# Running sums of an output projection loaded two blocks ahead, and a norm's product moved from VectorE to GpSimd

## The chip, the cores and the metric

The kernel runs on one core of a Trainium2 chip. The metric is the device time of one execution in microseconds (us); of several runs, the median counts. Engine names in the profile: PE is TensorE's matmul and PEld its weight load, DVE is VectorE, ACT is ScalarE, POOL is GpSimd, and SPq is the queue of SyncE, which issues the DMAs.

## What is computed

The reference is a two-layer decoder trunk on 1024 tokens of width 1024, in float32. Layer 0 is retention with 4 heads (query and key width 256, value width 512), layer 1 is stick-breaking attention with 8 heads (query and key width 128, value width 256) on keys and values that are made once from layer 0's result. Cut to what matters here:

```python
u = rms_norm(h, ret_norm_pre)
q, k, v, g = split(u @ ret_w_in)
q = rope(q, pos); k = rope(k, pos) * RET_QK_DIM ** -0.5
o = retention_chunkwise(q, k, v)                # per head
mu = mean(o, -1); var = mean(square(o - mu), -1)
o = (o - mu) * rsqrt(var + EPS)                 # the retention norm
y = (merge_heads(o) * silu(g)) @ ret_w_out      # the output projection
h = h + rms_norm(y, ret_norm_post)
k_sh, v_sh = split(rms_norm(h, kv_norm) @ w_kv)
# layer 1
q, g = split(rms_norm(h, sb_norm_pre) @ sb_w_in)
o = stick_breaking_attention(q, k_sh, v_sh)
y = (merge_heads(o) * silu(g)) @ sb_w_out
return h + rms_norm(y, sb_norm_post)
```

## The kernel before

The work is cut into four phases: retention on tokens 0 to 511 (A, t=0) and 512 to 1023 (A, t=1), then stick-breaking on the same halves (C, t=0 and t=1). A phase takes four heads, or four pairs of heads in C, one after the other. Every product of float32 matrices is made of three matmuls (`mm3`, lines 110 to 112) on high and low parts, which `split` (lines 254, 255, with a scale 257, 258) makes on ScalarE and VectorE. Weights come by DMA in tiles `wraw` of 128x512 and are split into `whl`.

The instructions are not ordered by hand to the last: steps of the main chain (projections) and side chains (scores, mixing, norm, statistics) are merged into one program by `merge`, and a scheduler then orders the instructions of each engine when the kernel is built, by the times it expects. All DMAs concerned are issued from SyncE's queue, in order: where one of them must wait for a tile or for a result, those behind it wait too. Tiles come from pools that rotate: a tile's memory is used again when its last reader is done. The pool `f2` has six buffers of 128x512; running sums, squares and the rotary's products use it. The PSUM banks of projections are two called `ma` and two called `mb`.

The output projection, `outproj`, is a chain of 16 steps: eight blocks `c` of 128 output columns, in two halves of 6 matmuls. Each head adds its part to running sums `y_d[c]` in DRAM. For the first head ScalarE copies the block from PSUM; for later heads the sum so far is loaded into an `f2` tile, VectorE adds the block (L194 in the profile) and the tile is stored. In the last output projection of a phase (except the last phase, which ends in another function) the block's squares are added up too, by ScalarE (L219, L222) and GpSimd (L223). The banks go ma, ma, mb, mb over the blocks; the projection that comes next takes all four at its first step. The three places where a phase's last output projection meets the next phase's first projection are called boundaries here: 1 is near 440 us, 2 near 862 us, 3 near 1283 us. In the last head of a retention phase the first four steps of the head before it (blocks 0 and 1) stand ahead of the projection of values and gates, the rest behind it.

The retention norm is in `mix`, step `o(ib)`, once for each of 4 heads, 4 blocks of 128 tokens and 2 halves, 32 times: statistics on VectorE (L608, L609), variance plus epsilon and its reciprocal root on GpSimd (L611, L612), the product -mean x root on VectorE (L613), and then `normed` on ScalarE (L625), which runs one step later for all but the last block and takes the root as scale and the product as bias. After that come the gate's multiply (L652), transposes on TensorE (L656) and a split. Rotary's last operations on GpSimd are L396 and L397; the row sums' loads and all other DMAs show as L64, the helper's line.

Of the kernel before, what the change touches and what calls it, by code (L numbers as in the profile page):

```python
# [13 lines left out]
ALU = mybir.AluOpType  # L14
# [17 lines left out]
def trunk(ctx, tc, xT, wts, gains, trig, ident_in, cols, out):  # L32
# [13 lines left out]
    def S(tag, shape, dt=F32):  # L46
        cnt[0] += 1
        return sb.tile([128] + list(shape), dt, tag=tag, name=f"{tag}{cnt[0]}", bufs=BUFS[tag])

    def PS(tag):  # L50
        cnt[0] += 1
        return ps.tile([128, 512], F32, tag=tag, name=f"p{tag}{cnt[0]}", bufs=BUFS[tag])
# [4 lines left out]
    def hl(tag):  # L57
        return S(tag, [2, 512], F32R)

    def f32(ap):  # L60
        return ap.bitcast(F32)

    def dma(dst, src, eng=nc.sync):
        eng.dma_start(dst.bitcast(F32), src.bitcast(F32))  # L64

    keep = tc.keep_in_program_order
    V, A_, G, MM = nc.vector, nc.scalar, nc.gpsimd, nc.tensor.matmul
# [28 lines left out]
    def unit(idx, gain=None):  # L96

        w = S("whl", [2, 1024], F32R)
        for c in range(2):
            o = 512 * c  # L100
            raw = S("wraw", [512])
            dma(raw[:], wts[idx, :, o:o + 512])
            for a, b, g in [(p[0] - o, p[1] - o, p[2]) for p in gain if o <= p[0] < o + 512] if gain else [(0, 512, None)]:
                split((w[:, 0, o + a:o + b], w[:, 1, o + a:o + b]), raw[:, a:b], g)
        return w

    def mm3(p, lh, ll, rh, rl, start, stop, goes_on=False):

        kw = dict(skip_group_check=True) if goes_on else {}
        MM(p, lh, rh, start=start, stop=False, **kw)  # L110
        MM(p, lh, rl, start=False, stop=False, **kw)  # L111
        MM(p, ll, rh, start=False, stop=stop, **kw)  # L112
# [19 lines left out]
    def ahead(n, make):  # L132

        box = {}

        def get(u):
            if u < n and u not in box:
                box[u] = make(u)
            return box.get(u)
        return get  # L140
# [28 lines left out]
    def outproj(base, oT, y_d, first, acc=None, tags=None):  # L169

        box = {}
        get = ahead(4, lambda ng: unit(base + ng))

        def chunk(j):
            c, half = divmod(j, 2)
            ng, b = divmod(c, 2)
            w = get(ng)
            if j % 4 == LEAD:
                get(ng + 1)
            if half == 0:  # L180
                box["p"] = PS(tags[c % 4] if tags and c < 4 else banks4[c % 4])
                box["y"] = S("f2", [512])
                if not first:
                    dma(box["y"][:], y_d[c])
            p, y = box["p"], box["y"]
            for e in (2 * half, 2 * half + 1):
                n = slice(256 * e + 128 * b, 256 * e + 128 * b + 128)
                mm3(p[:], w[:, 0, n], w[:, 1, n], oT()[e][:, 0, :], oT()[e][:, 1, :], e == 0, e == 3)
            if half == 0:
                return  # L190
            if first:
                A_.activation(y[:], p[:], AF.Copy)
            else:
                V.tensor_tensor(y[:], p[:], y[:], ALU.add)  # L194
            dma(y_d[c], y[:])
            if acc is not None:
                sumsq(acc, y[:], c)

        return Chunks([lambda j=j: chunk(j) for j in range(16)], lambda: get(0))

    def merge(main, *sides, nxt=None):
# [14 lines left out]
    def sumsq(acc, src, c):  # L216
        if c == 0:
            acc.append(S("acc", [512]))
            A_.activation(acc[0][:], src, AF.Square)  # L219
        else:  # L220
            t = S("f2", [512])
            A_.activation(t[:], src, AF.Square)  # L222
            G.tensor_tensor(acc[0][:], acc[0][:], t[:], ALU.add)  # L223
# [36 lines left out]
    def flat(x):  # L260
        return x[:, :, :].rearrange("p a b -> p (a b)")
# [3 lines left out]
    y_d = [[dr.tile([128, 512], F32, tag=f"y{t}{c}", name=f"y{t}{c}") for c in range(8)] for t in range(2)]  # L265
# [135 lines left out]
    class AHead:  # L401
# [139 lines left out]
        def out(self, y_d, acc=None, tags=None):  # L541
            return outproj(self.base + 12, lambda: self.oT, y_d, self.h == 0, acc, tags)
# [33 lines left out]
        def mix(self):  # L576

            h, q = self.h, self.q
            self.on, self.state = [], []

            def state_out(d):
                p = PS("o")
                for tb in range(4):
                    n, kn, v = slice(128 * d, 128 * d + 128), self.kn[tb], self.v[tb]
                    mm3(p[:], kn[:, 0, n], kn[:, 1, n], v[:, 0, :], v[:, 1, :], tb == 0, tb == 3)
                s = hl("ko")
                gg = GAMMA[h] ** HT
                A_.activation(s[:, 0, :], p[:], AF.Copy, scale=gg)
                V.scalar_tensor_tensor(s[:, 1, :], p[:], gg, f32(s[:, 0, :]), ALU.mult, ALU.subtract)
                dma(st_d[h][d][:], flat(s))  # L590

            def state_in():
                for d in range(2):
                    s = hl("ko")
                    dma(flat(s), st_d[h][d][:])
                    self.state.append(s)

            def o(ib):
                p = PS("o")
                il = slice(128 * ib, 128 * ib + 128)  # L600
                for d, s in enumerate(self.state):
                    mm3(p[:], q[d][:, 0, il], q[d][:, 1, il], s[:, 0, :], s[:, 1, :], d == 0, False)
                for jb in range(ib + 1):
                    n = slice(128 * (ib - jb), 128 * (ib - jb) + 128)
                    sc, v = self.sc[jb], self.v[jb]
                    mm3(p[:], sc[:, 0, n], sc[:, 1, n], v[:, 0, :], v[:, 1, :], not self.state and jb == 0, jb == ib)
                bs, mv = S("small", [6]), S("small", [2])
                V.bn_stats(bs[:], p[:])  # L608
                V.bn_aggr(mv[:], bs[:])  # L609
                r, nb = S("small", [1]), S("small", [1])  # L610
                G.tensor_tensor(r[:], mv[:, 1:2], cc[:, 16 + 4 * h + ib:17 + 4 * h + ib], ALU.add)  # L611
                G.tensor_tensor(r[:], r[:], mhalf[:, 0:1], ALU.pow)  # L612
                V.scalar_tensor_tensor(nb[:], mv[:, 0:1], -1.0, r[:], ALU.mult, ALU.mult)  # L613
                late.append((ib, p, r, nb))
                if ib:
                    normed()

            late = []

            def normed():  # L620
                ib, p, r, nb = late.pop(0)
                if ib % 2 == 0:
                    self.on2 = S("sgn", [1024])
                on = self.on2[:, 512 * (ib % 2):512 * (ib % 2) + 512]
                A_.activation(on, p[:], AF.Identity, scale=r[:], bias=nb[:])  # L625
                self.on.append(on)

            os = [lambda ib=ib: o(ib) for ib in range(4)] + [normed]
            if self.t == 0:
                self.give = [lambda d=d: state_out(d) for d in range(2)]  # L630
                return os
            self.give = []
            return [state_in] + os
# [94 lines left out]
    class CPair:  # L728
# [43 lines left out]
        def out(self, y_d, acc=None):  # L772
            return outproj(self.base + 12, lambda: self.oT, y_d, self.pr == 0, acc)
# [345 lines left out]
```

## Time and profile before

| what | value |
|---|---|
| runs | 1802.1, 1799.63, 1802.94 us; median 1802.1 |
| profiled execution, its own time | 1795.14 us |
| its span | 1793.4 us |
| mean granted TensorE clock | 0.994 |
| DMA moved | 292.14 MB, mean 163 GB/s |
| loads of running sums | 96, 256 KB each |

A line of the timeline gives the start, the length, the engine, the program's line, the operation, out<-in with the tiles' names, the shape, and in brackets the engine's idle time before it with the instruction or transfer that ended it. A line of the waits gives who waited, for whom, how many us in total, how many times, and the longest. A group's line gives busy us and mean ns of one, then the idle time before. A line of the windows gives, for a stretch of time, the busy us of each engine with the number of instructions, the granted clock as a share of full speed, and the share of the DMA engines. Durations come from one profiled execution. Matmuls are pipelined, so one of 0.39 us may follow another after 0.23.

### The profile page before, as it was taken

Reading aid. Unit: us, or ns where it says so; the run is one execution under the profiler, and the core shown is the slowest. Engines: PE = TensorE matmul, PEld = TensorE weight load, DVE = VectorE, ACT = ScalarE, POOL = GpSimd, SP = SyncE. Lnnn points to the kernel's source line nnn. Section 1 sums busy time; section 2 is a strip of 40 time slices with the busy share of each in tenths; the row PEclk is TensorE's granted clock in tenths of the full one; section 3 lists DMA queues with packets and bytes.
Section 4 is the critical chain, followed back from the end, with each engine's and each line's share of the span. In section 5 each row is a group of like instructions: output and inputs, shape, how many; then the busy total and the mean of one; then the engine's idle time right before and its main releaser. Section 6 shows DMA issues by size and latency. Waiting matters only on the chain. (4 is left out here: it accounts for less than half of the span.)

```text
span 1793.4 us, 23629 instructions
## 1 busy us (share of the span) xinstructions
PE 1736.5 (97%) x8132; PEld 1432.5 (80%) x8132; DVE 1197.1 (67%) x1947; ACT 815.8 (45%) x1526; POOL 266.5 (15%) x345
## 2 busy tenths in 40 slices
PE   8999999999999899999999999999999999999997
PEld 6888788777788688777777888888787888888886
DVE  7757767887866868697475455557577456646675
ACT  6435546464444535363344443444344445344541
POOL 0210302201304210101131100000200010000103
PEclk9999999999999999999999999999999999999998
DMA  5225465557445646275664526344644442522243
GB/s 190 83 106 194 147 235 177 182 194 265 158 140 196 216 147 232 92 251 188 213 216 158 199 80 200 129 153 152 220 144 166 139 144 94 174 97 102 98 136 112
DMA packets 152553, 292.14 MB, mean 163 GB/s; under 512 B 17136, under 2 KB 19312, under 8 KB 152432
## 3 DMA queue, kind: packets, MB, share of 16 engines
q1 hardware_dynamic: 152432, 290.63, 47.8%
q8 instruction: 64, 1.05, 0.2%
q14 instruction: 57, 0.47, 0.1%
HBM read 233.93 MB, written 56.62 MB: 162 GB/s over the span
## 5 line engine op out<-in xcount | busy, mean ns | idle before, releaser
L255 DVE TENSOR_TENSOR whl<-wraw,whl 128x512 fp32r<-128x512 f32 x312 | 219.7, 733 | 62.6 <-ACT whl L254 62.4
L254 ACT ACTIVATE whl<-wraw 128x512 fp32r<-128x512 f32 x312 | 183.5, 623 | 106.5 <-PE pmb L112 47.6
L258 DVE SCALAR_TENSOR_TENSOR whl<-wraw,gn,whl 128x256 fp32r<-128x256 f32 (+1 forms) x256 | 150.7, 633 | 117.2 <-ACT whl L257 114.4
L257 ACT ACTIVATE whl<-wraw,gn 128x256 fp32r<-128x256 f32 (+1 forms) x256 | 142.6, 611 | 151.2 <-PE pmb L112 121.1
L110 PE MATMUL pma<-xh,whl 128*128 128x512 f32 x384 | 154.8, 403 | 7.3 <-DVE f L194 6.8
L110 PE MATMUL pmb<-xh,whl 128*128 128x512 f32 x384 | 153.3, 399 | 2.1 <-DVE sg L768 1.4
L111 PE MATMUL pma<-xh,whl 128*128 128x512 f32 x384 | 150.9, 393 | 0.0
L112 PE MATMUL pma<-xh,whl 128*128 128x512 f32 x384 | 150.8, 393 | 0.0
L112 PE MATMUL pmb<-xh,whl 128*128 128x512 f32 x384 | 150.7, 393 | 0.0
L111 PE MATMUL pmb<-xh,whl 128*128 128x512 f32 x384 | 149.9, 390 | 0.0
L798 POOL TENSOR_SCALAR_AFFINE_SELECT sgn<-sgn 128x128 f32<-128x128 f32 x64 | 25.1, 392 | 671.8 <-ACT sgn L793 559.3
L800 DVE TENSOR_TENSOR_SCAN sgn<-sgn 128x128 f32<-128x128 f32 (+3 forms) x64 | 89.0, 1391 | 45.5 <-POOL sgn L798 45.5
L255 DVE TENSOR_TENSOR AT<-pz,AT 128x512 fp32r<-128x512 f32 (+1 forms) x96 | 53.0, 554 | 71.4 <-ACT AT L254 71.0
L254 ACT ACTIVATE AT<-pz 128x512 fp32r<-128x512 f32 (+1 forms) x96 | 46.7, 486 | 111.1 <-PE pz L830 111.0
L110 PEld LDWEIGHTS pma<-xh,whl 128*128 128x128 f32 x384 | 72.9, 190 | 22.6 <-DVE f L194 7.4
L110 PEld LDWEIGHTS pmb<-xh,whl 128*128 128x128 f32 x384 | 72.3, 188 | 17.8 <-DVE sg L768 3.1
L112 PEld LDWEIGHTS pma<-xh,whl 128*128 128x128 f32 x384 | 72.7, 189 | 16.0
L112 PEld LDWEIGHTS pmb<-xh,whl 128*128 128x128 f32 x384 | 72.2, 188 | 15.9
L111 PEld LDWEIGHTS pma<-xh,whl 128*128 128x128 f32 x384 | 72.9, 190 | 13.2
L111 PEld LDWEIGHTS pmb<-xh,whl 128*128 128x128 f32 x384 | 72.4, 188 | 13.5
L111 PE MATMUL pma<-oT,whl 128*128 128x512 f32 x208 | 81.5, 392 | 1.2 <-DVE oT L255 1.2
L110 PE MATMUL pma<-oT,whl 128*128 128x512 f32 x208 | 82.2, 395 | 0.4 <-DVE f L194 0.4
(310 smaller groups left out, 4485.3 us busy)
## 6 DMA issues: line engine op xcount, KB each, us to landing
wraw<-in_wts_dram SPq DMA_DIRECT2D x624, 256.0 KB, 3.2
y<-f SPq DMA_DIRECT2D x120, 256.0 KB, 2.9
f<-y SPq DMA_DIRECT2D x96, 256.0 KB, 3.6
v<-v SPq DMA_DIRECT2D x16, 512.0 KB, 3.2
vo<-v SPq DMA_DIRECT2D x32, 256.0 KB, 2.8
A<-h SPq DMA_DIRECT2D x12, 512.0 KB, 4.5
st<-ko SPq DMA_DIRECT2D x8, 512.0 KB, 3.7
sg<-in_xT_dram SPq DMA_DIRECT2D x16, 256.0 KB, 2.9
```

Of the source, the lines that this page charges most:

```text
L110: MM(p, lh, rh, start=start, stop=False, **kw)
L111: MM(p, lh, rl, start=False, stop=False, **kw)
L112: MM(p, ll, rh, start=False, stop=stop, **kw)
L254: A_.activation(dst[0], src, AF.Copy)
L255: V.tensor_tensor(dst[1], src, f32(dst[0]), ALU.subtract)
L257: A_.activation(dst[0], src, AF.Copy, scale=scale)
L258: V.scalar_tensor_tensor(dst[1], src, scale, f32(dst[0]), ALU.mult, ALU.subtract)
L798: G.affine_select(n[:, dg], n[:, dg], [[-1, 128]], ALU.is_gt, 1.0, base=0, channel_multiplier=1)
L800: V.tensor_tensor_scan(n[:, :W][:, ::-1], n[:, :W][:, ::-1], n[:, :W][:, ::-1], 1.0, ALU.mult, ALU.bypass)
```

## The change

`outproj` gets a helper, `sums`, that makes the tile of a block once and, where it is not the first head, starts its load. At the first half of block c, the tiles of blocks c, c+1 and c+2 are asked for, so a load is issued up to two blocks before its block's matmuls; before, it was issued at its own block's first half. For the first head nothing is asked ahead. In `mix`, VectorE now negates the mean right behind the statistics (new tile `nm`), and GpSimd multiplies it by the reciprocal root behind its power; the product on VectorE goes. VectorE issues as many instructions as before, GpSimd 32 more; numbers of matmuls and DMAs stay the same.

```diff
@@ outproj
+        def sum_so_far(c):
+            y = S("f2", [512])
+            if not first:
+                dma(y[:], y_d[c])
+            return y
+        sums = ahead(8, sum_so_far)
+
         def chunk(j):
...
             if half == 0:
                 box["p"] = PS(tags[c % 4] if tags and c < 4 else banks4[c % 4])
-                box["y"] = S("f2", [512])
+                sums(c)
                 if not first:
-                    dma(box["y"][:], y_d[c])
-            p, y = box["p"], box["y"]
+                    sums(c + 1)
+                    sums(c + 2)
+            p, y = box["p"], sums(c)
@@ mix, o(ib)
                 V.bn_stats(bs[:], p[:])
                 V.bn_aggr(mv[:], bs[:])
+                nm = S("small", [1])
+                V.tensor_scalar(nm[:], mv[:, 0:1], -1.0, None, ALU.mult)
                 r, nb = S("small", [1]), S("small", [1])
                 G.tensor_tensor(r[:], mv[:, 1:2], cc[:, 16 + 4 * h + ib:17 + 4 * h + ib], ALU.add)
                 G.tensor_tensor(r[:], r[:], mhalf[:, 0:1], ALU.pow)
-                V.scalar_tensor_tensor(nb[:], mv[:, 0:1], -1.0, r[:], ALU.mult, ALU.mult)
+                G.tensor_tensor(nb[:], nm[:], r[:], ALU.mult)
```

## The prediction

> **What bounds the kernel now.** I read the page first, then the waits of TensorE's weight loads, then the timelines around the rows that name a running sum, then the windows.
>
> ```profile
> span 1793.4 us, 23629 instructions
> PE 1736.5 (97%) x8132; PEld 1432.5 (80%) x8132; DVE 1197.1 (67%) x1947; ACT 815.8 (45%) x1526; POOL 266.5 (15%) x345
> ```
>
> TensorE is busy for 97% of the span, and the change takes no matmul away. So only TensorE's gaps, 1793.4 - 1736.5 = 57 us, and stretches at a lower clock can be won. The waits of the weight loads over the whole span say how many of those gaps belong to a running sum (columns: us in total, times, longest):
>
> ```profile
> PEld pma L110 <- DVE f L194: 8.4, 5, 2.8
> PEld pmb L110 <- DVE f L194: 1.0, 1, 1.0
> ```
>
> Six waits, 9.4 us, for the add at L194. The timeline of the weight loads (start, length, in brackets the idle time before it) and the waits between 1250 and 1320 us show where they are:
>
> ```profile
> 441.75 0.19 PEld L110 LDWEIGHTS pma<-xh,whl 128*128 128x128 f32 x1 [2.75 <-DVE f L194]
> 447.38 0.19 PEld L110 LDWEIGHTS pmb<-xh,whl 128*128 128x128 f32 x1 [1.00 <-DVE f L194]
> 862.03 0.19 PEld L110 LDWEIGHTS pma<-xh,whl 128*128 128x128 f32 x1 [1.03 <-issue]
> 866.83 0.19 PEld L110 LDWEIGHTS pma<-xh,whl 128*128 128x128 f32 x1 [2.19 <-DVE f L194]
> PEld pma L110 <- DVE f L194: 2.4, 1, 2.4
> ```
>
> These are the three phase boundaries: the last output projection of a phase, followed by the first projection of the next, which wants the same PSUM banks. Between them they hold 2.75 + 1.00 + 1.03 + 2.19 + 2.4 = 9.4 us. (The 1.03 has no releaser; it is the same wait for a bank, so I count it. Two small waits elsewhere make up the 8.4.)
>
> Why the adds are late there is in SyncE's queue and on VectorE:
>
> ```profile
> 431.68 0.32 SPq L64 DMA_DIRECT2D y<-f  x1
> 432.09 0.38 SPq L64 DMA_DIRECT2D f<-y  x1
> ...
> 436.05 0.69 DVE L194 TENSOR_TENSOR f<-pma,f 128x512 f32<-128x512 f32 x1 [1.71 <-DMA f<-y]
> 441.00 0.69 DVE L194 TENSOR_TENSOR f<-pma,f 128x512 f32<-128x512 f32 x1 [3.66 <-DMA f<-y]
> ...
> 450.64 0.69 DVE L194 TENSOR_TENSOR f<-pmb,f 128x512 f32<-128x512 f32 x1 [3.31 <-DMA f<-y]
> ```
>
> The load of a block's sum is issued right behind the store of the sum before it, and the add waits for that load. It is a ring: store issued at 431.68, load at 432.09, add at 436.05, next add at 441.00, 4.95 us a block. TensorE does a block in 12 matmuls:
>
> ```profile
> 424.52 0.39 PE L110 MATMUL pmb<-qk,whl 128*128 128x512 f32 x1
> ...
> 427.24 0.39 PE L110 MATMUL pma<-qk,whl 128*128 128x512 f32 x1
> ```
>
> These rows are 12 matmuls apart: 2.72 us a block. At 4.95 against 2.72 the adds fall behind, and TensorE pays at the end.
>
> **The sums, loaded two blocks ahead.** The number of loads does not change, only their place. In the changed kernel's build order, the load of block c+3 stands behind the store of block c at the three boundaries. From the end of block c's matmuls, the add (0.69 and some 0.2 to start), the store's issue (0.4) and the load (432.09 to 436.05, 3.96) take 5.2 us. The sum is wanted three blocks later, 3 x 2.72 = 8.16 us. Some 2.9 us are to spare, so the add follows its matmuls, and all five gaps go: **-9.4 us**. The build order there also returns to the plain one; before, two groups of the next projection's matmuls were put back behind others, since their banks were known to come late. What is late next is each block's own matmuls, which is TensorE itself. Elsewhere loads already stood far ahead, and adds waited for TensorE alone.
>
> One gap pair costs more than its length. The windows show it (columns: us, then busy time of PE, PEld, DVE, ACT, POOL with counts, granted clock, DMA share, GB/s):
>
> ```profile
> 864.31:867.73 3.42, 1.65 (x8) 1.04 (x7) 1.91 (x5) 0.63 (x1) 0.10 (x1) 1.00 0.29 107
> 867.73:871.14 3.41, 3.41 (x10) 2.64 (x9) 0.69 (x1) 0.33 (x1) 1.18 (x1) 0.50 0.66 218
> 942.83:949.65 6.82, 5.08 (x13) 3.49 (x12) 5.97 (x11) 4.94 (x12) 3.98 (x7) 0.50 0.73 258
> 460.00:480.00 20.00, 19.07 (x84) 15.31 (x83) 19.22 (x28) 9.16 (x17) 6.75 (x5) 1.00 0.46 155
> ```
>
> After a window in which TensorE was busy for 1.65 of 3.42 us, the clock granted is 0.50 for 3.41 us: half of it lost, 1.7 us. Without the gaps the dip goes: **-1.7 us**, between 0 and -1.7.
>
> [...]
>
> **Loads brought forward elsewhere.** In the last head of both retention phases the loads of blocks 2 and 3 now stand right behind those of blocks 0 and 1, on SyncE's queue, ahead of weight loads:
>
> ```profile
> 756.76 1.17 SPq L64 DMA_DIRECT2D f<-y  x2
> 761.37 2.62 SPq L64 DMA_DIRECT2D wraw<-in_wts_dram  x2
> 760.76 1.72 POOL L397 TENSOR_TENSOR f<-f,f 128x512 f32<-128x512 f32 x1
> ```
>
> The two moved loads need tiles of a six-deep ring that rotary's subtract and add on GpSimd (L396, L397) still read, so SyncE stands until about 760.76 + 1.72 = 762.5 and then spends two more issues. The weights of 761.37 slip by some 1.3 us, and so do the store of block 1 and the weights behind it. They are used some us later, so I take half of that for each of the two places, **+1.0 us** with rounding down, between 0 and +2.5. Nothing in it can gain.
>
> **The norm's product.** There are 32 such norms (4 heads, 4 blocks, 2 halves). The first one, on three engines:
>
> ```profile
> 86.91 0.18 DVE L609 BATCH_NORM_AGGREGATE small<-small 128x2 f32<-128x6 f32 x1
> 87.18 0.19 POOL L611 TENSOR_TENSOR small<-small,cc 128x1 f32<-128x1 f32 x1 [9.44 <-DVE small L609]
> 87.45 0.56 POOL L612 TENSOR_TENSOR small<-small,mhalf 128x1 f32<-128x1 f32 x1
> 88.04 0.16 DVE L613 SCALAR_TENSOR_TENSOR small<-small,small 128x1 f32<-128x1 f32 x1 [0.95 <-POOL small L612]
> 88.24 0.78 ACT L625 ACTIVATE sgn<-po,small,small 128x512 f32<-128x512 f32 x1 [3.71 <-DVE small L613]
> DVE small L613 <- POOL small L612: 32.8, 32, 4.1
> ```
>
> VectorE does statistics, waits for GpSimd's add and power, and multiplies; only then ScalarE starts. The last row, from the waits of the whole span, is what leaves VectorE: 32 waits, 32.8 us. It keeps 32 instructions, since the negation of the mean takes the place of the product, and that needs nothing from GpSimd. But VectorE is 67% busy, and idle time there counts only where TensorE waits behind it. The weight loads' waits between 380 and 405 us, and between 822 and 835 us (last row), give what lies in chains behind such a wait:
>
> ```profile
> PEld pmb L111 <- DVE whl L255: 1.5, 2, 1.0
> PEld pz L656 <- DVE qk L255: 1.3, 1, 1.3
> PEld pz L656 <- DVE qk L255: 1.2, 1, 1.2
> ```
>
> That is 4.0 us at most. A good part of each is the split's own work and ScalarE's, so I take less than half, **-1.5 us**, between 0 and -4.0.
>
> The price is a third instruction on GpSimd before ScalarE may start:
>
> ```profile
> L611 POOL TENSOR_TENSOR small<-small,cc 128x1 f32<-128x1 f32 x32 | 10.2, 320 | 276.6 <-DVE small L609 276.6
> L613 DVE SCALAR_TENSOR_TENSOR small<-small,small x32: 159/160/1294, 88.0 to 828.5; 128x1 f32<-128x1 f32 x32
> ```
>
> GpSimd's add of the same shape has a mean of 320 ns, VectorE's product a median of 160. In the first norm ScalarE starts at 88.24; with a power that ends at 88.01, a product as long as the add (0.19) and gaps of 0.08 in front and behind, it would start at 88.36, 0.1 later. If all 32 were on the path at the means, 32 x (0.320 - 0.160) = 5.1 us. Blocks are normed one step after they are made and TensorE has other work meanwhile, so I take **0**, between 0 and +5.1.
>
> [...]
>
> **The sum.** -9.4 - 1.7 + 1.0 - 1.5 = -11.6 us. The profiled execution took 1795.1 us, 1.7 more than its span; it would take 1783.5, a factor of 0.9935. It was shorter than each of the three runs shown (1799.6 to 1802.9). The same factor on their median, 1802.1, gives **1790.5 us**.
>
> **The rivals.** *GpSimd's product lies on the path.* All 5.1 us are paid: -6.5, 1795.6 us. For it: ScalarE's 0.78 us start right behind the product. Against it: TensorE's waits name this chain for few us.
>
> *Given back.* Where TensorE reaches the next stage early, that stage may not be ready. From 460 to 480 us VectorE is busy for 19.22 of 20 us, so it may take back boundary 1's 3.75 us. The window at 942.83, with the clock at 0.50, lies in a stage where TensorE waits for ScalarE (weight loads' waits, 850 to 960 us):
>
> ```profile
> PEld pz L110 <- ACT A L794: 5.3, 2, 2.8
> ```
>
> It may take back boundary 2's 3.2 and 1.7. What is left is -11.6 + 3.75 + 4.9 = -2.9, 1799.2 us. Against it: TensorE is still busy for 19.07 of those 20 us.
>
> *The sums stay late, and nothing covers them any more.* The load needs a tile of the six-deep ring, released among others by GpSimd's add at the boundary:
>
> ```profile
> 432.50 1.29 POOL L223 TENSOR_TENSOR acc<-acc,f 128x512 f32<-128x512 f32 x1 [3.73 <-ACT f L222]
> ```
>
> SyncE stands at it, with stores and weights queued behind. If the adds come no earlier than now, the plain order costs more than the one put back: TensorE starts the projection at 441.7, wants the last bank 2.7 us later at 444.4, and gets it at 450.64 + 0.69 = 451.3. The stall is 2.75 + 6.9 = 9.7 in place of 3.75, +5.9; for three boundaries +17.8, and with the +1.0 and -1.5 it gives 1819 us. It turns into a loss where TensorE's waits at a boundary exceed 3.75 us; the projection's first 2.7 us cover as much, so the last sum must land some 2.9 + 2.7 + 3.75 = 9.3 us later than I work out. Against it: L223's 1.29 us begin soon after the add, and GpSimd is 15% busy.
>
> *It changes little*: loads that are early already stay so; only the three boundaries are at stake, and that is what is summed.
>
> **The numbers.** The measurement can tell about 0.2%, 3.6 us, from no change: 1798.5 to 1805.7. The forecast has 0.68. Its own range by the terms' bounds is 1790.5 - 2.5 - 1.0 = 1787 (norm at -4.0, early loads at 0) to 1790.5 + 1.5 + 1.5 + 1.7 = 1795.2 (norm at 0, early loads at +2.5, the dip stays); the runs of before lie 3.3 us apart, so I give it 1785 to 1796. The product on the path has 0.10, given back 0.14, sums late 0.08. Faster takes the first two, 0.78; the same, given back, 0.14; slower 0.08. The range leaves out the late sums and a little at each end, and one more us for that spread: 1784 to 1800.
>
> **What would show it.** Right: waits for L194 vanish from the weight loads; adds at the boundaries 2.7 us apart; no clock of 0.50 near 868; VectorE waits for GpSimd gone at the norm, ScalarE waiting for GpSimd instead, 0.1 us later. Wrong: loads at the boundaries landing after their matmuls, new waits of TensorE for weights near 340 or 765, or a dip at a new place.

## The result, and the profile after

The changed kernel took 1785.2 us, the median of six runs (1782.84 to 1788.89), where the kernel before took 1802.5, the median of six (1795.71 to 1803.84). The ratio is 0.9911, with a 95% interval from 0.9892 to 0.9930: 16 us faster, with 1790.5 forecast. The profiled execution of after took 1788.89 us, the longest of its six; that of before, 1795.14, was not one of those six and is shorter than all of them. So the two traces lie only 6 us apart, and that will matter below.

The page, first lines:

```profile
span 1787.2 us, 23678 instructions
PE 1738.4 (97%) x8132; PEld 1436.5 (80%) x8132; DVE 1195.9 (67%) x1947; ACT 814.4 (46%) x1526; POOL 291.9 (16%) x377
```

TensorE is idle for 1787.2 - 1738.4 = 48.8 us, where it was 56.9. GpSimd is busy for 25 us more, though 32 products of some 0.2 us make only 6.8 of that; the last section comes back to it. Of the weight loads' waits for a running sum, 9.4 us before, one line is left:

```profile
PEld pma L110 <- DVE f L202: 0.4, 1, 0.4
```

VectorE's own waits for a loaded sum, over the whole span, were 25.9 us before, all of them at the three boundaries (first row), and are 2.0 now (second row; L202 is the old L194):

```profile
DVE f L194 <- DMA f<-y: 25.9, 11, 3.9
DVE f L202 <- DMA f<-y: 2.0, 1, 2.0
```

Boundary 1 on SyncE, VectorE's adds there, and boundary 3's last adds (timelines):

```profile
431.07 0.32 SPq L64 DMA_DIRECT2D y<-f  x1
431.49 0.38 SPq L64 DMA_DIRECT2D f<-y  x1
...
432.16 0.68 DVE L202 TENSOR_TENSOR f<-pma,f 128x512 f32<-128x512 f32 x1
434.14 0.69 DVE L202 TENSOR_TENSOR f<-pma,f 128x512 f32<-128x512 f32 x1 [1.29 <-PE pma L112]
436.94 0.64 DVE L318 TENSOR_TENSOR f<-S 128x256 f32<-128x256 f32 x1 [1.13 <-DMA y<-f]
440.46 0.68 DVE L202 TENSOR_TENSOR f<-pmb,f 128x512 f32<-128x512 f32 x1
441.66 0.68 DVE L202 TENSOR_TENSOR f<-pmb,f 128x512 f32<-128x512 f32 x1
...
1274.67 0.68 DVE L202 TENSOR_TENSOR f<-pmb,f 128x512 f32<-128x512 f32 x1
1276.68 0.69 DVE L202 TENSOR_TENSOR f<-pmb,f 128x512 f32<-128x512 f32 x1 [1.33 <-PE pmb L112]
```

The first two rows look like before: a store, and 0.4 us later a load. But the load is now for a block three further on, and no add in these rows waits for it. What ends VectorE's idle time before an add is TensorE (`PE pma L112`, `PE pmb L112`), as it should be.

Boundary 1 is not as clean as forecast, though. From 434.14 to 440.46 no sum is added. VectorE has gone on to the next phase's preparation (L318 to L321), which wants tiles of the same `f2` ring and waits twice for a store to land (`DMA y<-f`, 1.13 us here and 0.67 at L320); the rest of the time is that preparation's and the splits' own work, and two adds are queued behind it all. They end at 442.3. TensorE does not see it, because the next projection's first 2.7 us use the other two banks. That is a new wait, hidden with little to spare.

The norm, first instance, on three engines, and what VectorE now waits for at the gate (waits, whole span):

```profile
87.03 0.18 DVE L617 BATCH_NORM_AGGREGATE small<-small 128x2 f32<-128x6 f32 x1
87.25 0.15 DVE L619 TENSOR_SCALAR small<-small 128x1 f32<-128x1 f32 x1
87.57 0.56 POOL L622 TENSOR_TENSOR small<-small,mhalf 128x1 f32<-128x1 f32 x1
88.21 0.19 POOL L623 TENSOR_TENSOR small<-small,small 128x1 f32<-128x1 f32 x1
88.44 0.78 ACT L635 ACTIVATE sgn<-po,small,small 128x512 f32<-128x512 f32 x1 [3.78 <-POOL small L623]
DVE sgn L662 <- ACT sgn L635: 48.3, 27, 6.1
```

From the end of the statistics (87.21) to ScalarE's start are 1.23 us, where they were 88.24 - 87.09 = 1.15. VectorE's 32.8 us of waiting for GpSimd are gone. But before, the same gate line was

```profile
DVE sgn L652 <- ACT sgn L625: 19.0, 21, 2.1
```

so 29.3 of the 32.8 us came back as waiting for ScalarE, one step later in the same chain.

### The profile page after: what moved, and what is told of

The parts are those of the page before. It is cut to its first block, busy times and chain, and to the rows that moved or that the text cites. A ratio compares the mean times of both kernels' runs of the same rounds, so it can differ in the third digit from the quotient of the medians.

```text
span 1787.2 us, 23678 instructions
## 1 busy us (share of the span) xinstructions
PE 1738.4 (97%) x8132; PEld 1436.5 (80%) x8132; DVE 1195.9 (67%) x1947; ACT 814.4 (46%) x1526; POOL 291.9 (16%) x377
## 4 chain that ended last, share of the span: by engine, by line
issue 23%; PE 23%; DVE 7%; POOL 2%; DMA 2%; ACT 1%; SPq 0%; POOLq 0%; DVEq 0%; ACTq 0%
PE pma L110 3%; PE pmb L110 3%; PE pma L111 3%; PE pma L112 3%; PE pmb L112 3%; PE pmb L111 3%; DVE whl L263 1%; DVE sgn L810 1%; DMA vo<-in_xT_dram 1%; PE po L112 1%; PE po L111 1%; POOL sgn L808 1%; PE po L110 1%; DVE A L811 1%; PE pz L840 1%
## 5 line engine op out<-in xcount | busy, mean ns | idle before, releaser
L112 PE MATMUL pmb<-xh,whl 128*128 128x512 f32 x384 | 150.8, 393 | 0.0
L112 PE MATMUL pma<-xh,whl 128*128 128x512 f32 x384 | 150.6, 392 | 0.0
L112 PEld LDWEIGHTS pmb<-xh,whl 128*128 128x128 f32 x384 | 72.5, 189 | 16.0
L112 PEld LDWEIGHTS pma<-xh,whl 128*128 128x128 f32 x384 | 72.3, 188 | 15.8
```

## The experiments

Two theories stood against each other. A: the sums carry the gain, by the gaps at the boundaries and by the clock that is lost after gaps. B: VectorE, freed of its waits, carries what the forecast was short of. Medians and ratios are against runs of the kernel before on the same chip.

**The changed kernel again**, without an edit.

> The changed kernel once more, for its spread. The profiled executions differ by 6.2 us (span 1793.4 to 1787.2), the medians by 17.3. Theory A: the difference lies in half-clock stretches of 3.41 us, each worth up to 1.7 us and 0.00095 of mean granted clock, whose number differs from run to run; the profile of before shows 2 inside the work (one of double length), that of after 5. Then the spans of the runs follow the mean clock, about 1.7 us for 0.001, in both kernels, and before has more of such stretches on average (mean clock lower by some 0.003 to 0.004). Theory B: the clock explains nothing; runs of one kernel at equal mean clock still differ by 5 us and more, and the two kernels have the same mean clock on average. Both expect 0.989 to 0.993 of before.

Measured: 1786.7 us against 1801.5, ratio 0.9911 (0.9890 to 0.9932). The clock explains a part. Over all runs of this study whose clock was recorded, before has a mean granted clock of 0.9918 and a mean span of 1800.4 us (45 runs), the changed kernel 0.9937 and 1784.0 (12 runs). In both, spans fall as the clock rises, by about 0.9 to 1.1 us for 0.001, where 1.8 were to be had if every us counted. So of 16.4 us the clock makes at most 0.0019 x 1790 = 3.4 us, and about 2 by the slope. At equal clock the two kernels remain some 14 us apart: A's clock is real but small.

This second profile of the changed kernel also shows how little there is to spare at boundary 1: VectorE's waits for a tile are 2.03 and 0.87 us there, and TensorE does see the late adds (timeline of the weight loads):

```profile
443.73 0.19 PEld L110 LDWEIGHTS pmb<-xh,whl 128*128 128x128 f32 x1 [0.41 <-DVE f L202]
444.93 0.19 PEld L110 LDWEIGHTS pmb<-xh,whl 128*128 128x128 f32 x1 [0.67 <-DVE f L202]
```

**Only the sums.** The norm as before:

```diff
-                nm = S("small", [1])
-                V.tensor_scalar(nm[:], mv[:, 0:1], -1.0, None, ALU.mult)
...
-                G.tensor_tensor(nb[:], nm[:], r[:], ALU.mult)
+                V.scalar_tensor_tensor(nb[:], mv[:, 0:1], -1.0, r[:], ALU.mult, ALU.mult)
```

> Only the sums' loads two blocks ahead; the norm's product stays on VectorE. Theory A (the sums carry the gain: 9.4 us of gaps at three boundaries and the clock lost after them): 12 to 16 us under before, about 1788, and a mean clock as high as with the whole change. Theory B (VectorE freed from 32.8 us of waiting carries what the prediction was short of): 6 to 9 us under before, about 1795.

Measured: 1785.5 us, 0.9912 (0.9892 to 0.9932). It is the whole change's time, as far as intervals of 3 to 4 us to each side can tell. The sums carry the gain, and B, which expected about 1795, falls.

**Only the norm**, with the kernel before's loads.

> Only the norm's product on GpSimd; the sums are loaded as before. Theory A: VectorE's 32.8 us of waiting for GpSimd come back as waiting for ScalarE at the gate, so 0 to 3 us under before, about 1800, and the boundaries' waits for L194 unchanged at 8 to 10 us. Theory B: 7 to 10 us under before, about 1794. Rival of the prediction (product on the path): 3 to 5 us over before.

Measured: 1800.8 us against 1801.5, 0.9987 (0.9973 to 1.0002): not told apart from no change, and at most 5 us. The boundaries' waits are there in full (weight loads' waits), and two stretches at half clock begin right behind them (windows; the number behind POOL's column is the granted clock):

```profile
PEld pma L110 <- DVE f L194: 10.0, 5, 4.6
PEld pmb L110 <- DVE f L194: 0.2, 1, 0.2
443.43:450.26 6.83, 5.46 (x13) 4.31 (x14) 6.11 (x10) 1.89 (x3) 1.54 (x1) 0.50 0.67 237
873.51:876.92 3.41, 3.41 (x10) 2.62 (x8) 0.69 (x1) 0.21 (x1) 1.27 (x1) 0.50 0.71 228
```

In the trace of before only boundary 2 had one, of 3.41 us; here boundaries 1 and 2 have 10.24 us together. With gaps at the same places, which of them costs clock differs from execution to execution.

**One block ahead** in place of two, with the norm's change:

```diff
                     sums(c + 1)
-                    sums(c + 2)
```

> The whole change with the sums loaded one block ahead in place of two. By the prediction's working the load then stands behind the store of two blocks before: 5.2 us of store and load against 2 x 2.72 = 5.44 us, just in time, so no wait for L194 over 0.5 us at the boundaries and a time within 3 us of the whole change. If the work at a boundary is longer than that (a slot released late by GpSimd, a longer landing), waits of 1 to 2 us come back at each of the three, and it is 4 to 8 us slower than the whole change.

Measured: 1788.1 us, 0.9928 (0.9904 to 0.9952), 3 us over two blocks by the ratios, with intervals that overlap. At boundary 1 a wait is back (timeline of the weight loads), at the other two there is none over 0.5 us:

```profile
441.56 0.19 PEld L110 LDWEIGHTS pmb<-xh,whl 128*128 128x128 f32 x1 [1.45 <-DVE f L201]
```

Just in time was nearly right: one place of three was late by 1.45, and there one add had waited 1.1 us for its load.

**The kernel before, profiled again.**

> The kernel before, profiled once more. The prediction was made on an execution of 1795.1 us, where the median of seventeen is 1801.5. Theory A (that execution happened to have few half-clock stretches: idle times at the boundaries bring one whenever they fill about half of a 3.41 us window, and where the windows fall differs from run to run): this execution shows its boundary waits for L194 again at 8 to 11 us in total, and if its mean clock is near 0.991 to 0.992, half-clock stretches right behind boundary 1, 2 or 3 that the first profile did not have, each 3.4 or 6.8 us long. Theory B (the runs differ in waits or transfers): the boundary waits are longer by 4 us and more at the same clock.

Measured: span 1799.3 us at a clock of 0.995. Here the expected clock did not show, and theory A's reading of the first trace as one with little clock lost fails for this execution: it lost no more, and was 5.9 us longer. But where it lost clock is in line with A: the first stretch at half clock inside the work begins right behind boundary 3, where the first trace had none (windows).

```profile
1289.38:1292.79 3.41, 3.41 (x10) 2.64 (x9) 1.73 (x2) 0.63 (x1) 0.93 (x2) 0.50 0.76 243
```

A gap of 2.48 us came before it; the gap of 3.88 us at boundary 1 of the same execution cost no clock. So each of the three profiles without early loads has such a stretch behind at least one boundary, the first profile of the changed kernel has none there, and the length of the gap alone does not decide it. Nor does the share of idle time that theory A goes by: in the 3.41 us ahead of each stretch inside the work of the first traces of before and after, TensorE is busy for 0 to 1.97 us, but it is busy for only 1.77 from 437.65 us in before and 1.72 from 209.49 us in after, with no stretch behind (windows):

```profile
437.65:441.06 3.41, 1.77 (x8) 1.13 (x6) 0.06 (x1) 1.15 (x2) 1.25 (x1) 1.00 0.88 273
441.06:444.47 3.41, 2.72 (x12) 2.26 (x13) 3.41 (x6) 0.67 (x2) 1.56 (x1) 1.00 0.84 308
209.49:212.90 3.41, 1.72 (x9) 1.11 (x8) 3.41 (x4) 2.19 (x5) 1.84 (x2) 1.00 0.21 77
212.90:216.31 3.41, 3.41 (x20) 2.87 (x19) 3.41 (x7) 1.20 (x2) 0.00 (x0) 1.00 0.63 216
```

The boundary waits (weight loads' waits) were a little longer than in the first:

```profile
PEld pma L110 <- DVE f L194: 10.5, 5, 3.9
PEld pmb L110 <- DVE f L194: 1.0, 1, 1.0
```

That is 2.1 of the 5.9 us; matmul by matmul (by the starts of the same matmul in both traces) the rest comes in steps of 0.4 to 1.6 us over the span, up and down. These two executions of one kernel lie 6 us apart by many small waits and two stretches at half clock, not by one thing; the runs of this kernel lie up to 13 us apart (1794.6 to 1807.8).

**Ahead at the boundaries only.** The other output projections load at their own block again:

```diff
-                if not first:
+                if acc is not None:
                     sums(c + 1)
                     sums(c + 2)
```

> The whole change, but sums are loaded ahead only in the last output projection of a phase; in the others each load stays at its own block. This takes back the loads brought forward in the last head of the retention phases. By the prediction's term (+1.0, between 0 and +2.5) it is 0 to 2.5 us under the whole change, about 1784.5. If the early loads cost nothing because the delayed weights are used later: no difference that can be told, within 2 us of the whole change. In both cases no wait for L202 over 0.5 us at the boundaries, and 0.989 to 0.993 of before.

Measured: 1786.2 us, 0.9913 (0.9897 to 0.9928). No difference from the whole change that can be told: the gain is at the three boundaries, and the early loads elsewhere neither bring nor cost more than the intervals of about 3 us hide. The traces say more. In the changed kernel (SyncE's timeline) the four loads hold the queue near 755 us, and the next weights come 6.16 us behind the first of them, where the rows in the prediction have 761.37 - 756.76 = 4.61 and this run 4.61 again:

```profile
754.65 6.06 SPq L64 DMA_DIRECT2D f<-y  x4
760.81 0.38 SPq L64 DMA_DIRECT2D wraw<-in_wts_dram  x1
```

So the slip that the prediction forecast is there, 1.55 us. But TensorE's waits at that place, 1.16, 1.28, 0.67 and 0.41 us, are the same with the slip and, to 0.01 us, without it.

**Three blocks ahead**, with one more line `sums(c + 3)`.

> The whole change with the sums loaded three blocks ahead. Theory A (two blocks leave 2.9 us to spare, so nothing is left to win): within 2 us of the whole change. The prediction's rival (loads hold the six-deep ring, SyncE stands at a tile that is released late, weights and stores are queued behind): waits of TensorE for weights or for L194 of 1 to 5 us come up at the boundaries or in the last head of the retention phases, 2 to 10 us over the whole change.

Measured: 1794.0 us, 0.9957 (0.9942 to 0.9973): half the gain is lost. TensorE's order at boundary 1 is that of two blocks ahead, and there it stands (timeline of the weight loads, VectorE's timeline, window):

```profile
445.49 0.19 PEld L110 LDWEIGHTS pmb<-xh,whl 128*128 128x128 f32 x1 [3.81 <-DVE f L203]
...
444.76 0.68 DVE L203 TENSOR_TENSOR f<-pmb,f 128x512 f32<-128x512 f32 x1
...
446.57:449.98 3.41, 3.29 (x8) 2.62 (x9) 3.10 (x3) 1.15 (x3) 2.29 (x2) 0.50 0.97 335
```

The add at 444.76 is the one that came at 440.46 with two blocks. 4.3 us later, it is no longer hidden by the 2.7 us of the other banks: a stall of 3.81 and one of 0.67 us for the next bank, and half a clock for 3.41 us behind it. Matmul by matmul, 5.7 of the 8.3 us between this profile and the changed kernel's are lost here. VectorE waited 1.35 us for a tile that GpSimd's sum of squares held (`POOL acc L232`), 11 us before the late add. This is kin to the forecast's rival of late sums, at a lead of three, with VectorE standing at the tile in place of SyncE.

**Three blocks ahead, seven tiles**, to see whether the ring is what holds it (the first diff line; the others make room):

```diff
-                ... f2=6, ...
+                ... f2=7, ...
-    ones = sb.tile([128, 128], F32, name="ones")
-    V.memset(ones[:], 1.0)
+    ones = f32(onesr)
```

> Sums three blocks ahead as in the run before that lost 8 us to two blocks ahead, with seven tiles in the pool in place of six (made as in the run with seven tiles and two blocks). In the profile of three blocks and six tiles, TensorE stands 3.81 us at boundary 1 for an add that is queued on VectorE, behind work whose tiles wait for GpSimd's adds of squares. Theory A (the tiles of the ring run out): with one more, the 3.81 us and the half-clock stretch behind them go, and the time is within 2 us of the whole change. Rival (loads too early crowd SyncE's queue or VectorE's order, tiles do not matter): still 0.994 to 0.997 of before.

Measured: 1788.0 us, 0.9922 (0.9910 to 0.9935). Most of the loss is gone; of the 3.81 + 0.67 us at boundary 1, 0.93 is left, and VectorE waits for no tile there. By the times, whose intervals lie apart, the tiles were the cause. The trace alone would not show it: TensorE reached this boundary 3.4 us later than with six tiles, for waits that came before, and the late add comes at nearly the same time (444.58). **Two blocks ahead with seven tiles**, the same edit on the changed kernel:

> The whole change with seven tiles in the pool of running sums and squares in place of six (the room comes from the tile of ones, which is now one with its rounded copy, and a shorter tile of gains). Theory A (at two blocks ahead, tiles come free in time): within 2 us of the whole change, that is 0.990 to 0.992 of before. Rival (tiles already bind at two blocks): 2 to 6 us under it.

Measured: 1786.1 us, 0.9911 (0.9897 to 0.9925). No gain: at two blocks the wait for a tile is there, but hidden.

**A longer chain on GpSimd**: four more products behind the product, with the whole change.

```diff
-                G.tensor_tensor(nb[:], nm[:], r[:], ALU.mult)
+                nb1 = S("small", [1])
+                G.tensor_tensor(nb1[:], nm[:], r[:], ALU.mult)
+                for _ in range(3):
+                    G.tensor_tensor(nb1[:], nb1[:], ones[:, 0:1], ALU.mult)
+                G.tensor_tensor(nb[:], nb1[:], ones[:, 0:1], ALU.mult)
```

> The whole change, with four more dependent GpSimd products of the same shape behind the product in each of the 32 norms (by a column of ones, so the value stays). By rows of the changed kernel's profile one takes 0.19 us, and 0.08 lies between two: ScalarE's norm starts some 1.1 us later each time, 35 us in all. Theory A (the norm is made one step after its block, TensorE has other work meanwhile): under a quarter of that comes through, 0 to 8 us over the whole change. Rival (the product lies on the path): 25 to 35 us over it.

Measured: 1805.0 us, 1.0018 (1.0007 to 1.0029). That is 1.0018 - 0.9911 = 0.0107, or 19 us over the whole change for 35 us of chain: neither theory. Some 3 of the 19 go with the clock, whose mean over these runs is 0.9904 against 0.9937, by the slope above. The loss comes in a few lumps, at the ends of heads, where the last block's norm has no step behind it. The transposes that follow it, in the timelines of the weight loads of this kernel and of the changed one (second row):

```profile
215.99 0.72 PEld L670 LDWEIGHTS pz<-ident,sgn 128*128 128x128 f32 x4 [5.39 <-DVE oT L263]
```

```profile
212.63 0.42 PEld L666 LDWEIGHTS pz<-ident,sgn 128*128 128x128 f32 x4 [2.12 <-DVE oT L263]
```

A longer chain of 4 x 0.27 = 1.1 us in each of four blocks made 3.3 us more wait here, and 6.83 us at half clock begin at 213.04, which the changed kernel's profile does not have there. So about half of what is put into this chain comes out in time, the clock included; the product is not free, it is only short.

## Why the prediction held, point by point

**The sums, -9.4 us: right, and the main part.** Waits for L194 were 9.4, 10.2 and 11.5 us in three executions without early loads, and 0.4, 1.4, 0.4 and 0.6 in the four with two blocks ahead and six tiles. Sums alone gave the whole gain, loads ahead at the boundaries alone as well. TensorE's idle time (span less busy) was 56.9, 61.1 and 58.2 us in the three, and 48.8, 50.8, 48.8 and 49.8 in the four: about 9 less. And the gain lies where it was forecast: matmul by matmul, the profile after gains 3.5, 4.6 and 2.3 us on that of before at boundaries 1, 2 and 3, 10.4 in all with the clock behind boundary 2, where the prediction's rows gave 3.75, 3.2 + 1.7 and 2.4. The second profiles of the two kernels part by 10.8 us at the same three places.

**5.2 us against 8.16 us, 2.9 to spare: right in outcome, incomplete in mechanism.** The loads are early enough. But at boundary 1 two adds come 4 and 2 us after their matmuls all the same, since VectorE stands for a tile of the ring and then has other work queued ahead of them; the sign "2.7 us apart" failed there. I had tied the tile only to SyncE's loads; it held VectorE's queue, by the next phase's preparation. The rival that I gave 0.08 was therefore nearer than I thought: one more block of lead, and it cost half the gain.

**The clock, -1.7 us: mis-sized.** I counted the one stretch of the one trace. The runs' mean clocks put the whole term between 2 and 3.4 us. The profile after lost more clock than that of before (0.992 against 0.994), in five stretches away from the boundaries. By the prediction's own signs a dip at a new place speaks against it. But these came behind waits that the kernel before has too (two of them shorter there, 1.79 against 2.43 us and 2.80 against 4.07), as in the window of 1339.30 to 1342.71 us behind a gap of 2.14 us (first row); the kernel before has the same gap and no stretch behind it (second row, weight loads):

```profile
1339.30:1342.71 3.41, 3.41 (x10) 2.63 (x9) 2.30 (x4) 0.50 (x1) 0.00 (x0) 0.50 0.68 240
1346.27 0.42 PEld L830 LDWEIGHTS pz<-ident,A 128*128 128x128 f32 x4 [2.15 <-DVE AT L255]
```

So whether a gap costs clock differs between executions, and a trace shows one draw. The stretches inside the work are of 3.41 or 6.83 us, behind differing gaps of the same kernel, and within the first profile of each kernel they start whole multiples of 3.413 us apart: in that of before from 867.73 to 942.83, which is 22 of them, in that of after from 318.72 to 595.20, which is 81, and from there to 762.45, which is 49.

**Early loads, +1.0 us: not shown.** The weights slipped by 1.55 us, about as forecast, but TensorE's waits near 760 us did not grow; near 344 us its wait for a split weight is 0.56 and 0.98 us in the two profiles of before and 1.07 and 0.65 in the two of after. The time cannot tell 1.0 us from nothing (0.9913 with the loads taken back, 0.9911 without).

**The norm, -1.5 us: nothing that can be told on top of the sums** (0.9912 without, 0.9911 with), and alone some 2 us, with an interval from a gain of 5 to none. The step that failed is that relief of VectorE's 32 waits reaches TensorE: 29.3 of 32.8 us came back at the gate, and TensorE's waits in this chain, from which the 1.5 was to come, did not shrink (`pz` for `qk`, 2.5 us before and 2.8 after). And the product's price of 0 was right only as a balance, since about half of a longer chain shows. Its bound of 5.1 us set the mean of GpSimd's add (320 ns) against the median of VectorE's product (160 ns), a factor of two; the means are 320 and 229, the medians 191 and 160, and the moved product takes 212 in the mean. So a factor of two is not what these tiles of one column show. In both forecast and trace ScalarE starts 0.1 us later in the first norm.

**The rest.** Forecast -11.6, measured 16; 1785.2 lies only 1.2 us inside the low end of the range, 1784 to 1800. Of 16.4 us between the mean spans, the boundaries make 10 to 11, with the clock lost right behind them. Some 5 to 6 are not accounted for by any trace here; clock lost elsewhere may be a part, and the rest stays open. The two profiled executions of before were shorter than its mean span. That the total came out no further off is in part luck: +1.0 and -1.5 were both too large and cancelled in part.

**The rivals.** The product on the path and the given-back gain did not show in the time. Near 470 us, where I feared for boundary 1's gain, TensorE's waits are those of before. Behind boundary 2, matmul by matmul, 4.6 us gained by 873 us became 3.6 by 965: 1.0 given back, not 4.9.

## What to carry to other kernels

Where a read-add-store loop runs behind matmuls, compare its period (load + add + store's issue, here 4.95 us) with the matmuls of a block (here 2.72). With each load behind a store on one queue, a lead of two blocks took the waits for the sums here from 9.4 us to 0.4; a third block took tiles from others and gave back half the gain (0.9957 against 0.9911, and 0.9922 with one tile more). Judge a relieved wait by what the same engine waits for next in the same chain, before counting it as gain: here 29.3 of 32.8 us came back there. And when the expected effect is under one per cent, profile the same kernel twice before reading a term from one trace: the two of the kernel before lie 5.9 us apart.

## What was not expected of the hardware

With the product moved, GpSimd's power became slower in the mean, though number and shape are the same. The groups (busy us, mean ns) of the kernel with the sums alone, and of the changed one:

```profile
L620 POOL TENSOR_TENSOR small<-small,mhalf 128x1 f32<-128x1 f32 x32 | 17.5, 548 | 2.5
L622 POOL TENSOR_TENSOR small<-small,mhalf 128x1 f32<-128x1 f32 x32 | 23.2, 725 | 2.5
```

With the norm alone it is at 741. The mean hides what happens: the median stays 548 ns. In the trace after, 26 of the 32 take 0.54 to 0.57 us as before, and six take 0.67 to 2.15. The same norm in the kernel before (first two rows, GpSimd and VectorE) and after (last two):

```profile
184.06 0.55 POOL L612 TENSOR_TENSOR small<-small,mhalf 128x1 f32<-128x1 f32 x1
184.65 0.16 DVE L613 SCALAR_TENSOR_TENSOR small<-small,small 128x1 f32<-128x1 f32 x1 [0.71 <-POOL small L612]
```

```profile
184.61 2.15 POOL L622 TENSOR_TENSOR small<-small,mhalf 128x1 f32<-128x1 f32 x1
184.47 1.88 DVE L263 TENSOR_TENSOR whl<-wraw,whl 128x512 fp32r<-128x512 f32 x3
```

Before, VectorE stood still until the power was done. Now it goes on with three splits, each with two inputs in SBUF, the on-chip memory, and the power ends at 186.76 us, 0.41 behind the last of them. In all six long ones VectorE works on such pairs from the power's start on. At 391.40 and 807.16 us, where it adds to the contents of a PSUM bank instead (L202, L508), the power takes 0.54 and 0.55. That VectorE's pairs are what makes the six long is my estimate from these instances; no run changed the pairs alone.

The mask on GpSimd (L575, L567 in the kernel before) went from a mean of 886 to 1263 ns between the same two profiles, but that is not the change's doing: the second profile of the kernel before has it too (second row).

```profile
L575 POOL TENSOR_SCALAR_AFFINE_SELECT sc<-sc 128x256 fp32r<-128x256 f32 x32 | 40.4, 1263 | 120.6 <-DVE sc L263 116.3 <-ACT f L504 4.0
L567 POOL TENSOR_SCALAR_AFFINE_SELECT sc<-sc 128x256 fp32r<-128x256 f32 x32 | 38.0, 1187 | 122.4 <-DVE sc L255 122.2
```

In both, one mask of 10.43 us makes most of the difference, where the shortest takes 0.41. So of the 25 us that GpSimd is busy for longer in the first trace, the product (6.8) and the power (5.7) are the change's, some 12 us over 32 norms.
